# Four of a convolution's 31 taps as products with diagonal matrices

## The chip, the cores and the metric

The kernel runs on one core of a Trainium2 chip. The metric is the device time of one execution in microseconds, median of three runs.

## The reference

Two layers of a transformer for 512 latent and 256 context tokens of 1024 features, in float32. Each layer has a mixer, an output projection with a norm, and a mixture of 32 experts. The first layer's mixer is an attention beside a convolution module, and it is in that module that the change lies:

```python
def _conv_module(u, conv_w, conv_b, ln_g, ln_b):
    a, gate = jnp.split(u, 2, axis=-1)
    glu = a * jax.nn.sigmoid(gate)
    y = lax.conv_general_dilated(glu, conv_w[:, None, :], window_strides=(1,),
                                 padding=[(CONV_WIDTH // 2, CONV_WIDTH // 2)],
                                 dimension_numbers=('NWC', 'WIO', 'NWC'),
                                 feature_group_count=B_WIDTH) + conv_b
    ...
    return jax.nn.silu(yn)
```

Each of the 512 channels is convolved with 31 taps of its own (CONV_WIDTH is 31, B_WIDTH 512), for the latent tokens and the context's; a layer norm over the channels follows.

## The kernel before

Channels lie on the partitions, 128 to a channel tile, four tiles. The tokens of a tile are 784 columns: 512 latent, a gap of 16 zeros, 256 context. A tap is one instruction over 784 columns. Of the 31 taps of a tile, VectorE takes 20 (L746, the first, which also writes the bias, and 19 times L749, which multiplies and adds onto `acc`). The last 11 are products on ScalarE (L756, L759) that GpSimd adds up in `part` (L760); VectorE adds `part` onto `acc` at the end (L768).

The taps are work that fills gaps. `Conv` keeps two lists, `v` for VectorE's taps and `p` for the others, in the order of the channel tiles. `fill(nv, np)` takes so many from the front of each. It is called at fixed points of the program, whatever stands at the front of the lists.

The order of each engine's instructions is the program's own in the stages around the change; a planner orders three engines only in the first layer's output projection and in the second layer's attention (`FREE`). The stages are these.

- `mixer_ab_in`, the loop over the channel tiles (`for ct in range(1, 4)`): TensorE computes the gate of a tile (`ug`, 48 products), ScalarE its sigmoid, TensorE the input (`uu`, 48 products), and VectorE multiplies the two (`glu_of`, L919 and L920), which also puts the tile's taps into the lists (`conv.add`). Four calls `conv.fill(3, 1)` stand in each turn. The same loop splits the pages of weights for the next products: ScalarE writes a rounded high part (L290), VectorE the rest (L295). Channel tile 0 is done before the loop.
- The projection of queries, keys and values, token tile by token tile (`proj`, L695): a tile's products go to PSUM, then a chain on three engines norms, rotates and splits them (`qk_norm`, `qk_rotate`: L347 to L383) and TensorE transposes them a tile later (`qk_trans`). Calls of `fill` stand before the first tile (4), in each `qk_norm` (2) and after each `qk_rotate` (1).
- The first layer's attention (`Attention`): 24 units of two heads by one tile of 128 queries, units 0 to 7 of context tiles, 8 to 23 of latent ones. In each of the first 18 units VectorE takes 1 or 2 taps in turn, between the maxima of the scores (L493) and the scaling of the probabilities (L512). Each second unit also has the products of a chunk of the modulation (`gemv`, L189, L198).

PSUM holds two buffers of 1024 columns (`big`), which `ug`, `uu`, the projections (`qps`) and the attention's scores (`S`) take in turn, and four of 512 (`sm`). The tiles of split keys have the tag `ks` and two buffers, which in the stage before hold two tables (`iota`, `tri`).

Of the kernel before, what the change touches and what calls it, by code (L numbers as in the profile page):

```python
# [7 lines left out]
F32 = mybir.dt.float32  # L8
# [21 lines left out]
PTAPS = 11  # L30
GAP = TAPS // 2
# [8 lines left out]
# engines that do not keep the program's order, by region: 3 is the first layer's output projection, 6 the second's attention  # L40
FREE = {3: [PE, mybir.EngineType.DVE, POOL], 6: [PE, mybir.EngineType.DVE, POOL]}
# pages of the experts' first weights that a layer loads ahead: before the gate, and then at three points of its start
G1 = 3
FIRST = ((11, 0, 2), (7, 3, 2))
# pages beside the lasting ones that a layer's experts have: from the output projection on, and from the experts on
NT = (9, 11)
NS = (9, 3)
# chunks of the second layer's modulation: the tiles at which two are loaded, and how many the attention begins with
M1 = (4, 5)
M2 = 2  # L50
# the row block of the output projection after which the pages that were free before it are taken
# [17 lines left out]
def hybrid_dit_kernel(ctx: ExitStack, tc: tile.TileContext, a, out):  # L69
# [7 lines left out]
    def by_hand(r):  # L77
        """All engines but those given keep the program's order; those take what is ready first."""
        engines = set(ENGINES) - set(FREE.get(r, ()))
        if engines != held[-1]:  # L80
            held.append(engines)
            sched.close()
            sched.enter_context(tc.manual_schedule(engines=engines))
# [13 lines left out]
    class Pages:  # L97
        """Places of 4 KB a partition for weights and other data, each held by one tile after another: what is rounded
        for TensorE's one-pass products and what is not are tiles of their own."""
# [26 lines left out]
    def load(src, n=4, pools=None, queue=nc.sync):  # L126
        """The first n pages of a chunk of weights"""
        w = [pages.new("w", pools=pools) for _ in range(n)]
        for i in range(n):
            queue.dma_start(w[i], src[i])  # L130
        return w

# [31 lines left out]
    def warm(func):  # L164
        """Has ScalarE load the function's table ahead of its use"""
        nc.scalar.activation(keep.tile([128, 1], F32, tag="warm", name="warm", bufs=1), zeros, func)
# [14 lines left out]
    roomy = []  # L181

    def gemv(l, ch, w):
        """Products of a chunk of 512 columns; four column groups of the array take a row block each."""
# [18 lines left out]
    def gemv_first(n, w):  # L203
        """The shift and the scale of a pair of row blocks in layer 0's first norm"""
# [19 lines left out]
    def scale_cols(l, which):  # L224
        """ln gain * (1 + scale), one column a block of 128"""
# [8 lines left out]
    def mod_rows(l, name, src):  # L234
        """A vector of columns as rows in DRAM, to be read into all partitions."""
# [9 lines left out]
    def router_bias(l):  # L245
        """The router's logits of the second norm's shift, and its bias"""
# [12 lines left out]
    def rpow(work, ss, n, scale):  # L259
        """1/sqrt(ss * scale + eps)"""  # L260
# [14 lines left out]
    # A float32 is the sum of two parts of 12 bits each, which TensorE multiplies exactly in one pass each;  # L275
    # a product of two float32 takes three passes then: high * high, high * low and low * high.
    class Split:
        """A chunk of weights in its two parts, made page by page by the steps"""
# [20 lines left out]
        def __call__(self, p, k, o, n):  # L299
            """Columns o to o + n of row block k, part p"""  # L300
            per = PAGE // self.width
            o += k % per * self.width
            return self.parts[p][k // per][:, o:o + n]
# [6 lines left out]
    rope = {}  # L310

    def rope_tables(l, pool, t0=0, n=XT):
        """Of tiles t0 to t0 + n"""
# [17 lines left out]
    # Queries and keys are kept split: a query's two parts below one another on 128 partitions, a key's high part  # L331
    # twice and its low part twice, so that two passes over 128 rows give all four products.
    def qk_norm(l, t, ps, withq, v, work, room=None, fill=lambda n: None):
        """The values of a tile, from the projection in PSUM, and its queries and keys, normed."""
# [21 lines left out]
    def qk_rotate(l, t, n0, qn, W, mid):  # L356
        """Rotation and split of the normed queries and keys"""
# [28 lines left out]
    def keys_of(KS, n):  # L386
        """The tiles that hold the keys of token n, its place there, and how many of the four kinds each holds"""
# [4 lines left out]
    def qk_trans(t, parts, QS, KS):  # L392
        """[token, head dims] -> [head dims, token]"""
# [15 lines left out]
    class Attention:  # L409
        """Units (pair of heads j and j + 4, tile of queries t), three of them in flight: the scores of one,  # L410
        the transposition of the previous one's probabilities, the values of the one before."""
# [47 lines left out]
        def out(self, j, t):  # L459
            """A page holds two tiles of tokens."""  # L460
# [84 lines left out]
    class OutProj:  # L545
        """X += g1 * (feat^T @ w_out), the rms norm of that and the router's logits, tile by tile: a tile's norm
        and logits, and the next tile's features, run beside the products of the tile between them."""
# [89 lines left out]
        def chain_b(self, t, s):  # L637
            """The tile's new rows, transposed, with the second norm's gain"""
# [16 lines left out]
        def chain_c(self, t, s):  # L655
            """The logits: the norm's factor comes after the products, and its shift is in the bias."""
# [6 lines left out]
        def rows_a(self, t, s, eng):  # L663
            """The rows that the experts gather: in layer 0 with the gain and shift, in layer 1 without"""
# [15 lines left out]
    def modulate_T(l, r, h, ps, dst):  # L680
        """Half h of the transposed rows: the second norm's gain and shift, a column of them a block."""
# [9 lines left out]
    def proj(ps, h, tk, w, o, n, ks=range(KT)):  # L691
        """ps[:, o:o+n] = h^T @ w for a tile of tokens"""
# [36 lines left out]
    def col0(t):  # L729
        """A token tile's place among the convolution's columns"""  # L730
        return t * 128 if t < XT else NX + SEP + (t - XT) * 128

    class Conv:
        """The depthwise convolution as work that fills the gaps of VectorE and, for the last PTAPS taps,
        of ScalarE (products) and GpSimd (sums)."""

        def __init__(self, work, glu, acc):
            self.work, self.glu, self.acc = work, glu, acc
            self.v, self.p, self.part, self.started = [], [], {}, set()

        def add(self, ct):
            acc, glu, w = self.acc[:, ct, :], self.glu, lambda i: convp[:, ct, i:i + 1]

            def first():
                self.started.add(ct)
                nc.vector.tensor_scalar(acc, glu[:, ct, 0:CW], w(0), w(TAPS), op0=OP.mult, op1=OP.add)  # L746
# [4 lines left out]
            def ptap(i):  # L751
                if i == TAPS - PTAPS:
# [3 lines left out]
                    nc.scalar.activation(self.part[ct], glu[:, ct, i:i + CW], AF.Copy, scale=w(i))  # L756
# [4 lines left out]

            self.v += [first] + [lambda i=i: tap(i) for i in range(1, TAPS - PTAPS)]
            self.p += [lambda i=i: ptap(i) for i in range(TAPS - PTAPS, TAPS)]

# [86 lines left out]
    def mixer_ab_in(work, mr, xn, hi, v, glu, conv):  # L851
# [33 lines left out]

        tps = {}
# [40 lines left out]
        # channel tile 0, as the blocks of h come  # L927
# [51 lines left out]
        for ct in range(1, 4):  # L979
            w = w0 if ct < 2 else w1  # L980
            ps = big("ug")
            mm_u(ct, 1, ps, w, range(KT))
            conv.fill(3, 1)
# [16 lines left out]
            if ct == 3:  # L1000
                for f in wq.steps:
                    f()
            conv.fill(3, 1)
            glu_of(ct, ps, sig)
# [129 lines left out]
    class Router:  # L1134
        """Each tile's two experts a token and their places among the experts' tokens, tile by tile"""
# [70 lines left out]
        def finish(self):  # L1206
            """The rows that the experts' places take, and where their results go; out of bounds for an empty place,
            as a tile's number is less 64"""
# [16 lines left out]
        def weights(self, work):  # L1225
            """Each assignment's weight: the softmax of the group's logits at their maximum, times that of the two
            experts' logits"""
# [13 lines left out]
        def slots(self, pool, work, room):  # L1241
            """The token and the weight of each place: the tokens of pairs of experts one below the other, those of single
            experts in both halves; out of range and zero for an empty place"""
# [11 lines left out]
            # a weight in three parts of 8 bits, for products in bfloat16 with the places' rows of zeros and a one  # L1255
# [25 lines left out]
        def split(self, pool, w, tok, name):  # L1281
            """Leaves in w the weights of tokens and takes out those of the context's"""
# [6 lines left out]
    # An expert's tokens are taken in blocks of 64: block 0 always, block 1 where the expert has more than 64  # L1289
    # tokens, and the rest, if any expert has more than 128, in a loop of as many steps as that takes.  # L1290
# [22 lines left out]
    class Experts:  # L1313
# [13 lines left out]
        def ahead(self, most=None, spare=0, queue=nc.sync):  # L1327
            """Loads the weights in the order of their use, as far as there are places, but for the spare ones."""
# [27 lines left out]
        def scatter(self, n, b):  # L1356
            """The rows of a block's results, times weight and gate, added to the rows of their tokens. A token's two
            experts are of one group, and order goes round the groups: only every fourth expert can meet a row again."""
# [24 lines left out]
        def scaled(self, dst, yy, w, c):  # L1383
            """Column half c of a block's results, times weight and gate"""
# [7 lines left out]
        def result(self, n, yy):  # L1392
            """The results of an expert's first block, the pair's experts one below the other"""
# [775 lines left out]
```

## Time and profile before

| | |
|---|---|
| median of three runs | 1769.0 us (1768.14 to 1769.58) |
| the profiled execution's span | 1769.0 us |
| TensorE busy | 1567.2 us |
| VectorE busy | 913.2 us |
| ScalarE busy | 528.4 us |
| GpSimd busy | 427.4 us |
| mean granted TensorE clock | 0.966 of full speed |

The profile is of one execution. Engines are PE (TensorE, with PEld its weight loads), DVE (VectorE), ACT (ScalarE), POOL (GpSimd) and SP (the queue that issues most loads). A busy time counts an instruction from its start to its end; matmuls overlap, so a busy TensorE is not one at its peak. In rows of instructions a time in square brackets is the engine's idle time before the instruction, with what ended it. A product of two float32 operands that are not rounded stands as two matmul records.

### The profile page before, as it was taken

Reading aid. Unit: us, or ns where it says so; the run is one execution under the profiler, and the core shown is the slowest. Engines: PE = TensorE matmul, PEld = TensorE weight load, DVE = VectorE, ACT = ScalarE, POOL = GpSimd, SP = SyncE. Lnnn points to the kernel's source line nnn. Section 1 sums busy time; section 2 is a strip of 40 time slices with the busy share of each in tenths; the row PEclk is TensorE's granted clock in tenths of the full one; section 3 lists DMA queues with packets and bytes.
Section 4 is the critical chain, followed back from the end, with each engine's and each line's share of the span. In section 5 each row is a group of like instructions: output and inputs, shape, how many; then the busy total and the mean of one; then the engine's idle time right before and its main releaser. Section 6 shows DMA issues by size and latency. Waiting matters only on the chain. (4 is left out here: it accounts for less than half of the span.)

```text
span 1769.0 us, 24713 instructions
## 1 busy us (share of the span) xinstructions
PE 1567.2 (89%) x8732; PEld 866.9 (49%) x8732; DVE 913.2 (52%) x1747; ACT 528.4 (30%) x1036; POOL 427.4 (24%) x347
## 2 busy tenths in 40 slices
PE   5979689997899999998986789989799999989997
PEld 4867457885333333332321676677334344343442
DVE  3897889788333232322333656656534445344454
ACT  3422468733111111111112434663312122121221
POOL 1535556132112112211111223201121121111110
PEclk9999799999999999999999899999799999999999
DMA  9121743447999999999998338145699999999992
GB/s 368 58 83 66 292 155 122 164 148 278 354 396 397 388 390 386 391 394 389 392 400 332 123 108 319 58 180 188 257 408 408 408 408 406 408 406 406 405 407 91
DMA packets 151597, 519.03 MB, mean 293 GB/s; under 512 B 22445, under 2 KB 23181, under 8 KB 151437
## 3 DMA queue, kind: packets, MB, share of 16 engines
q1 hardware_dynamic: 134300, 479.67, 69.2%
q0 software_dynamic: 11520, 16.81, 3.7%
q10 hardware_dynamic: 5616, 20.45, 3.0%
q8 instruction: 97, 1.59, 0.4%
q14 instruction: 64, 0.52, 0.1%
HBM read 510.49 MB, written 21.02 MB: 300 GB/s over the span
## 5 line engine op out<-in xcount | busy, mean ns | idle before, releaser
L1476 PE MATMUL gu<-w,xt 128*64 128x512 f32 x2304 | 516.7, 597 | 21.1 <-DMA w<-in_ex_dram 11.9
L1476 PEld LDWEIGHTS gu<-w,xt 128*64 128x64 f32 x2304 | 171.5, 137 | 326.6 <-issue 247.6
L1500 PE MATMUL yy<-w,ht 128*64 128x512 f32 x1152 | 264.8, 601 | 14.2 <-PEq L1296 5.9
L1482 DVE TENSOR_TENSOR hh<-hh,gu 128x512 f32<-128x512 f32 x64 | 44.1, 688 | 451.6 <-ACT hh L1481 451.6
L1481 ACT ACTIVATE hh<-gu 128x512 f32<-128x512 f32 x64 | 38.3, 598 | 566.2 <-PEq L1296 416.2
L1500 PEld LDWEIGHTS yy<-w,ht 128*64 128x64 f32 x1152 | 81.4, 137 | 172.4 <-issue 133.7
L1379 POOL DMA_INDIRECT xD<-ys,sidx x40 | 70.6, 1765 | 317.8 <-DVE ys L1375 315.3
L1409 POOL TENSOR_TENSOR lo<-ys,hi 64x1024 fp32r<-64x1024 f32 x29 | 68.2, 2351 | 325.0 <-ACTq L1296 325.0
L749 DVE SCALAR_TENSOR_TENSOR acc<-glu,convp,acc 128x784 f32<-128x784 f32 x76 | 97.9, 1288 | 1.6
L760 POOL TENSOR_TENSOR part<-part,prod 128x784 f32<-128x784 f32 x40 | 84.7, 2118 | 43.2 <-ACT prod L759 42.2
L1375 DVE TENSOR_TENSOR ys<-yy,ys 128x512 f32<-128x512 f32 x64 | 44.3, 692 | 97.8 <-PEq L1296 53.4
L1408 ACT ACTIVATE hi<-ys 64x1024 fp32r<-64x1024 f32 (+1 forms) x35 | 34.4, 983 | 193.1 <-DVE ys L1386 108.8
L1352 POOL DMA_INDIRECT Xg<-hD,gidx x40 | 42.6, 1066 | 188.9 <-PE xtp L1460 179.7
L264 POOL TENSOR_TENSOR rs<-ms,mhalf 128x1 f32<-128x1 f32 (+2 forms) x40 | 41.5, 1038 | 170.8 <-DVE ms L262 170.3
L1390 DVE TENSOR_TENSOR X<-X,cmb 128x512 f32<-128x512 f32 x126 | 77.0, 683 | 1.6 <-PE cmb L1426 1.1
L1426 PE MATMUL cmb<-hi,oh 128*128 128x512 f32 x128 | 58.0, 453 | 22.2 <-DVE oh L1413 20.5
L1460 PEld LDWEIGHTS xtp<-cst,Xg 128*128 128x128 f32 x512 | 58.0, 146 | 34.6 <-PEq L1296 18.6
L1460 PE MATMUL xtp<-cst,Xg 128*128 128x128 f32 x512 | 64.8, 282 | 9.1 <-PEq L1296 9.1
L522 PE MATMUL ptp<-cst,P 128*128 128x128 f32 x368 | 53.3, 284 | 18.7 <-POOL P L510 10.5
L1494 DVE COPY ht<-htp 128x512 f32<-128x512 f32 x64 | 43.8, 684 | 50.0 <-PE htp L1489 50.0
L695 PE MATMUL qps<-wh,hi 128*128 128x256 f32 (+1 forms) x176 | 61.4, 349 | 8.0 <-DVE hi L1819 2.4
L687 DVE TENSOR_SCALAR xt<-xtp,A,modT 128x128 f32<-128x128 f32 x128 | 49.6, 410 | 35.7 <-ACT xt L689 34.6
(310 smaller groups left out, 2633.9 us busy)
## 6 DMA issues: line engine op xcount, KB each, us to landing
w<-in_ex_dram SPq DMA_DIRECT2D x751, 512.0 KB
w<-in_mod_w_dram SPq DMA_DIRECT2D x96, 512.0 KB
w<-in_ex_dram ACTq DMA_DIRECT2D x17, 512.0 KB
w<-in_w_out_dram SPq DMA_DIRECT2D x16, 512.0 KB
w<-in_w_in_ab_dram SPq DMA_DIRECT2D x14, 512.0 KB
hD<-x ACTq DMA_DIRECT2D x8, 512.0 KB
xD<-X ACTq DMA_DIRECT2D x6, 512.0 KB
w<-in_w_in_cd_dram ACTq DMA_DIRECT2D x6, 512.0 KB
```

Of the source, the lines that this page charges most:

```text
L522: nc.tensor.transpose(ps[:, (c - c0) * 128:(c - c0 + 1) * 128], u["P"][c // nk][:, c % nk * 128:(c % nk + 1) * 128], ident)
L687: nc.vector.tensor_scalar(dst[:, k, :], src, g, b, op0=OP.mult, op1=OP.add)
L695: nc.tensor.matmul(ps[:, o:o + n], h(x, k, tk), w(p, k, 0, n), start=(k == 0 and c == 0), stop=(k == KT - 1 and c == 2))
L749: nc.vector.scalar_tensor_tensor(acc, glu[:, ct, i:i + CW], w(i), acc, OP.mult, OP.add)
L760: nc.gpsimd.tensor_tensor(self.part[ct], self.part[ct], t, OP.add)
L1379: return nc.gpsimd.indirect_dma_start(out=xD[:, :], out_offset=bass.IndirectOffsetOnAxis(ap=idx, axis=0), in_=ys[:, :], in_offset=None, bo ...
L1390: nc.vector.tensor_tensor(x, x, ps, OP.add)
L1409: eng.tensor_tensor(lo[rows, c], ys[rows, c], hi[rows, c].bitcast(F32), OP.subtract)
L1426: nc.tensor.matmul(ps, oh[:, tok(t)], y[:, c * 512:(c + 1) * 512], start=(i == 0), stop=(i == 1))
L1460: nc.tensor.transpose(ps[:, k * 128:(k + 1) * 128], src[:, (h * 4 + k) * 128:(h * 4 + k + 1) * 128], ident)
L1476: nc.tensor.matmul(self.gu[c * 64:(c + 1) * 64, b, :], xt[:, k, q * 64:(q + 1) * 64], w[k][:, c * 512:(c + 1) * 512], start=(k == 0), stop ...
L1500: nc.tensor.matmul(yy[c * 64:(c + 1) * 64], t[:, b, f % 2, f // 2, :], w[f][:, c * 512:(c + 1) * 512], start=(f == 0), stop=(f == 3))
```

## The change

Of VectorE's 20 taps of a channel tile, taps 1 to 4 (`ETAPS`) become products on TensorE. For each tap ScalarE writes a diagonal matrix, the identity scaled by the tap's 128 weights, into a tile of the tag `ks` (`diag`, when the channel tile's taps are put into the lists). TensorE multiplies the four diagonals with the shifted columns and accumulates in a `big` buffer (`cps`), 8 products a channel tile. The first vector instruction, before a scalar form that wrote tap 0 and the bias, now multiplies tap 0 and adds the products' sum from PSUM. The bias goes into the first of the other 11 taps, on ScalarE.

The products are issued by `conv.early()`. In the loop this stands behind the gate products of the next channel tile; and the first vector instruction of a tile calls it for what is still unissued. Further, the last `conv.fill(3, 1)` of each turn of the loop is put behind `glu_of` instead of ahead of it. The other lines of the diff only take out comments.

```diff
+ETAPS = 4
...
-            self.v, self.p, self.part, self.started = [], [], {}, set()
+            self.v, self.p, self.e, self.ps, self.part, self.started = [], [], [], {}, {}, set()
...
+            diag = self.room.tile([128, 128 * ETAPS], F32, tag="ks", name="diag", bufs=2)
+            for i in range(ETAPS):
+                nc.scalar.activation(diag[:, tok(i)], ident, AF.Copy, scale=w(i + 1))
+
+            def products():
+                ps = self.ps[ct] = big("cps")
+                for o, n in ((0, 512), (512, CW - 512)):
+                    for i in range(ETAPS):
+                        nc.tensor.matmul(ps[:, o:o + n], diag[:, tok(i)], glu[:, ct, i + 1 + o:i + 1 + o + n], start=(i == 0), stop=(i == ETAPS - 1))
+
             def first():
                 self.started.add(ct)
-                nc.vector.tensor_scalar(acc, glu[:, ct, 0:CW], w(0), w(TAPS), op0=OP.mult, op1=OP.add)
+                self.early()
+                nc.vector.scalar_tensor_tensor(acc, glu[:, ct, 0:CW], w(0), self.ps.pop(ct)[:, 0:CW], op0=OP.mult, op1=OP.add)
...
-                    nc.scalar.activation(self.part[ct], glu[:, ct, i:i + CW], AF.Copy, scale=w(i))
+                    nc.scalar.activation(self.part[ct], glu[:, ct, i:i + CW], AF.Identity, bias=w(TAPS), scale=w(i))
...
-            self.v += [first] + [lambda i=i: tap(i) for i in range(1, TAPS - PTAPS)]
+            self.e.append(products)
+            self.v += [first] + [lambda i=i: tap(i) for i in range(ETAPS + 1, TAPS - PTAPS)]
             self.p += [lambda i=i: ptap(i) for i in range(TAPS - PTAPS, TAPS)]
+
+        def early(self):
+
+            while self.e:
+                self.e.pop(0)()
...
+        conv.room = work
...
             mm_u(ct, 1, ps, w, range(KT))
+            conv.early()
             conv.fill(3, 1)
...
+            glu_of(ct, ps, sig)
             conv.fill(3, 1)
-            glu_of(ct, ps, sig)
```

## Rows read from the trace of the kernel before

**Rows 1.** The page's first part: busy time, share of the span, instructions of each engine.

```profile
PE 1567.2 (89%) x8732; PEld 866.9 (49%) x8732; DVE 913.2 (52%) x1747; ACT 528.4 (30%) x1036; POOL 427.4 (24%) x347
```

**Rows 2.** Busy us by stretch: PE, PEld, DVE, ACT, POOL; granted clock, DMA share, GB/s.

```profile
94.00:116.00 22.00, 15.94 (x80) 13.62 (x79) 21.57 (x19) 7.31 (x9) 8.05 (x4) 0.84 0.00 0
...
260.00:280.00 20.00, 20.00 (x190) 15.47 (x183) 19.56 (x31) 16.86 (x35) 9.28 (x7) 1.00 0.57 213
460.00:900.00 440.00, 421.39 (x2036) 152.38 (x2032) 129.52 (x192) 67.08 (x110) 82.46 (x55) 1.00 1.03 393
```

**Rows 3.** TensorE's timeline, 67 to 134 us: start, duration, line, tiles, idle before.

```profile
67.54 0.51 PE L910 MATMUL uu<-hi,wh 128*128 128x512 f32 x2
...
85.40 0.61 PE L910 MATMUL uu<-hi,wh 128*128 128x512 f32 x2 [0.87 <-DVE glu L920]
...
108.57 1.01 PE L910 MATMUL uu<-hi,wh 128*128 128x512 f32 x2 [6.06 <-DVE glu L920]
...
120.70 0.49 PE L695 MATMUL qps<-wl,hi 128*128 128x512 f32 x1 [1.32 <-DVE wl L295]
...
128.12 0.50 PE L695 MATMUL qps<-wh,hi 128*128 128x512 f32 x1 [1.85 <-DVE glu L920]
...
133.77 0.28 PE L695 MATMUL qps<-wh,hi 128*128 128x256 f32 x1
```

**Rows 4.** VectorE, 60 to 135 us: its taps as a group, then its timeline.

```profile
L749 DVE SCALAR_TENSOR_TENSOR acc<-glu,convp,acc 128x784 f32<-128x784 f32 x34 | 47.5, 1398 | 1.0
...
60.91 0.69 DVE L746 TENSOR_SCALAR acc<-glu,convp 128x784 f32<-128x784 f32 x1
61.63 2.10 DVE L749 SCALAR_TENSOR_TENSOR acc<-glu,convp,acc 128x784 f32<-128x784 f32 x2
...
81.14 3.27 DVE L749 SCALAR_TENSOR_TENSOR acc<-glu,convp,acc 128x784 f32<-128x784 f32 x3
...
85.26 6.21 DVE L749 SCALAR_TENSOR_TENSOR acc<-glu,convp,acc 128x784 f32<-128x784 f32 x3
...
132.14 2.35 DVE L295 TENSOR_TENSOR wl<-w,wh 128x1024 fp32r<-128x1024 f32 x2
```

**Rows 5.** TensorE's timeline at two plain float32 products.

```profile
259.61 1.92 PE L189 MATMUL mps<-w,silu_c 128*32 128x512 f32 x16
...
1116.87 1.09 PE L1978 MATMUL py<-q,pw 128*128 128x512 f32 x2
```

**Rows 6.** Timeline of TensorE and VectorE in the projection.

```profile
141.91 0.51 PE L695 MATMUL qps<-wh,hi 128*128 128x512 f32 x1 [2.32 <-DVE qn L353]
...
162.09 0.95 PE L198 MATMUL mpt<-cst,mrows 128*128 128x2 f32 x8
...
164.17 0.47 PE L695 MATMUL qps<-wh,hi 128*128 128x512 f32 x1
...
165.90 1.03 DVE L749 SCALAR_TENSOR_TENSOR acc<-glu,convp,acc 128x784 f32<-128x784 f32 x1
...
171.50 0.82 DVE L353 TENSOR_TENSOR qn<-qps,rs 128x640 f32<-128x640 f32 x1 [0.79 <-POOL rs L264]
...
195.54 0.77 PE L482 MATMUL S<-low,hi 128*128 128x256 f32 x2 [8.66 <-DVE room L353]
```

**Rows 7.** Attention: a group of VectorE's (227 to 290 us); timeline at units 5, 10, 15, 18.

```profile
L749 DVE SCALAR_TENSOR_TENSOR acc<-glu,convp,acc 128x784 f32<-128x784 f32 x16 | 22.9, 1430 | 0.2
...
196.24 3.64 PE L189 MATMUL mps<-w,silu_c 128*32 128x512 f32 x16
...
226.38 0.75 DVE L493 TENSOR_REDUCE nm<-S 128x1 f32<-128x256 f32 x2
...
257.86 1.80 DVE L493 TENSOR_REDUCE nm<-S 128x1 f32<-128x768 f32 x2
...
285.91 1.81 DVE L493 TENSOR_REDUCE nm<-S 128x1 f32<-128x768 f32 x2
...
302.44 1.82 DVE L493 TENSOR_REDUCE nm<-S 128x1 f32<-128x768 f32 x2 [0.65 <-PE S L482]
```

## What the change will do to the time: the prediction

> **What bounds the kernel now.** The page first: TensorE is busy for 89% of the span and VectorE for 52% [rows 1]. Averages say little about a change in one stretch, so the windows come next. The experts' stretch, from 460 us on, is bound by its weights: the DMA engines are busy throughout [rows 2]. The convolution lies before it. Three stages hold it: the loop over the four channel tiles of the gated input (59 to 128 us), the projection of queries, keys and values (128 to 195), and the first layer's attention (195 to 337). I see nothing that would absorb a shift of these: what the attention's end loses or wins I pass on whole.
>
> In the loop VectorE is the bound. From 94 to 116 us it is busy for 21.57 of 22 us, and TensorE for 15.94 at a granted clock of 0.84 [rows 2]. TensorE's timeline shows it waiting for VectorE four times, 0.87, 6.06, 1.32 and 1.85 us, three times for the gating product that frees a PSUM buffer and once for a page of split weights [rows 3]. So one expects that taking taps from VectorE pays here. But the change does not take them from this loop.
>
> **Where the taps go.** The vector taps are a list, taken from the front at fixed points: 36 in the loop (three rounds of 12), 21 in the projection (4, 2 and five times 3), the rest in the attention. Before, the list has 4 x 20 = 80 entries, so 23 fall to the attention; afterwards 4 x 16 = 64, so 7. Both earlier stages issue as many vector instructions as before. All 16 that go leave the attention: its units 0 to 4 still take 1, 2, 1, 2, 1, and units 5 to 15 take none.
>
> **Price of the products.** Each channel tile gains four products of 512 columns and four of 272, in plain float32. No such accumulating set is in the trace. The nearest: the pool's product of 128 x 128 by 512 columns, one product in two records, 1.09 us with its tail; and the modulation's 16 records, four abreast, 1.92 us, so 0.48 a record with the tail and some 0.43 without [rows 5]. By 0.43: 4 x 2 x 0.43 x (1 + 272/512) = 5.3 us a tile. Upper bound 6.7 (1.09 for each 512), lower 2.6 (one record each); I take 5.3, the nearest row being the same kind of operand. Building the diagonals is 16 ScalarE copies of 128 x 128; ScalarE is busy for 7.31 of 22 us [rows 2] and stands idle after the gate's sigmoid, so they cost nothing; without that cover they'd be about 1 us a tile.
>
> **The loop.** The first vector instruction of tile 0 began at 60.91 [rows 4], and VectorE then worked without a pause. Now it reads the products. Those stand in TensorE's order behind the whole gate batch of the next channel tile, which ended at 67.54 [rows 3], so they end at 67.5 + 5.3 = 72.8. All engines keep the program's order here, and so VectorE stands still for 11.9 us with two split pages, nine taps and the next gating behind it. That is the main cost of the change. Tiles 1 and 2 don't repeat it: their first instruction is 16 and 32 entries down the list, by which time their products are done.
>
> What it costs is bounded from both sides. If VectorE stays the bound, the queue up to the key/value weights' split (ended at 134.5 [rows 4]) comes 11.9 us later, and about 1 more because three first instructions run where two did, without the scalar form's 0.69 us against a tap's 1.05 [rows 4]: +12.9. From this goes contention: three taps took 3.27 us where GpSimd had only small work and 6.21 beside its long additions, and the loop's 34 taps took 47.5, not 34 x 1.05 = 35.7 [rows 4]. Two or three additions now run while VectorE stands, about 1 us each; so +10. If TensorE is the bound: from 67.54 to the key/value product at 133.77 it spent 66.2 us, of which 10.1 waiting and about 2 lost at half clock (the pair after the long wait took 1.01 us, its like 0.61) [rows 3]; 54.1 of work plus 3 x 5.3 is 70.0, +3.8. But it will also wait about 4 us in the second tile's gate batch, whose last split pages VectorE now delivers late: +7.8. Between 7.8 and 10 I take **+8.5** (bounds +3.8 and +12.9). Issuing three taps behind each gating product removes the 6.06 us wait, and that is in these sums.
>
> [...]
>
> **The projection.** VectorE, ScalarE and GpSimd pass one tile after the other through a serial chain, and TensorE follows it (it waited 2.32 us for the normed queries at 141.9 [rows 6]). The fourth channel tile's products are not issued in the loop; the first instruction of tile 3 issues them, entry 49, taken while the fourth token tile is projected. TensorE reaches them at 162.1 by the clock of before and ends at 167.4; the instruction that needs them stood at 165.90 [rows 6]. The diagonals also hold one of two buffers from which the key tiles are split, so that tile's keys wait for the same 167.4. The chain loses 1.5 to 2.6 us; I take **+2.6**. A product tile also takes one of two PSUM buffers; if the fifth projection gets the one freed at about 169 it waits for nothing, TensorE itself being there 2.1 us behind the products (164.17 against 162.09 before [rows 6]), at 169.5.
>
> **The attention.** The 16 taps took 22.9 us of VectorE [rows 7], but not all was in the way. Units 10 to 15 (257.86 to 285.91) took 5.6 us each with taps, units 15 to 18 5.5 without [rows 7], and TensorE was busy for 20.00 of 20 us [rows 2]: nothing to win. Units 5 to 9 took 31.5 us and held eight of the sixteen taps, 11.4 us at their mean of 1.43 [rows 7]. Without them a unit still waits for ScalarE's exponentials, GpSimd's scaling behind its own additions, and TensorE's modulation product; following the queues I find about 0 in unit 5, 1.2 in 6, 1.4 in 7, 0.8 in 8 and 1.8 in 9, where the row vectors' DMA chain starts earlier: **-5.2** (bounds 0 and -11.4; -22.9 if VectorE bounds it all). TensorE waited 8.66 us before the attention [rows 6], and the first modulation product ran at half clock, 3.64 against 1.92 us [rows 5, 7]; the wait falls to about 4. Whether the clock then falls no row says: 6.06 and 8.66 were followed by it, 2.32 was not [rows 3, 6]. I take half: **-0.9**.
>
> **Sum.** The profiled span is 1769.0, as is the median of the three runs. 1769.0 + 8.5 + 2.6 - 5.2 - 0.9 = **1774.0 us**.
>
> **Rivals.** *VectorE was what bound the whole attention.* For it: its queue shows no gap between units 10 and 15. Against: TensorE's full windows and the equal pace of units 15 to 18. If 20 of the 22.9 us come back: 1769 + 11.1 - 20 - 0.9 = 1759. It decides the sign when the attention gives back over 11; chance 0.13, over 1759 to 1765.
>
> *The loop hides the stall.* VectorE catches up and TensorE's sum alone counts: +3.8, and the chain +1.5, the attention -6: 1768. For it: the 10 us of waits that go. Chance 0.25, 1766 to 1771. The change then does nothing that can be measured.
>
> *The buffers turn strictly.* The fifth projection then waits for the fourth tile's queries (171.50 + 2.6 + 0.8 = 174.9 instead of 169.5 [rows 6]); some 3.2 of these 5.4 reach the chain's end: 1777. If the clock halves in the new waits (the loop's 6.06 us wait cost about 2 that way), 1779 to 1781. [...] Chance 0.17.
>
> **How the numbers follow.** My forecast, 1771 to 1777, has 0.45. A measurement of this kernel tells 0.2%, 3.5 us, from no change. Slower than 1772.5: three quarters of the forecast (0.35) and the buffers' 0.17, 0.52. Within: the rest and most of the hidden stall, 0.34. Faster: 0.14. The range for 8 in 10 leaves out the far part of the attention rival and the worst of the clock: 1764 to 1780.
>
> **What would show it.** Right: VectorE idle for about 12 us from 61 us on until products that start near 67.5; product sets of 5.3 us; no 6 us wait before the third gating; the key/value projection starting near 142; keys of the fourth token tile waiting for products; units 5 to 9 some 5 us shorter and units 10 to 15 as long as before. Wrong: products that begin before the gate batch, units 10 to 15 below 5 us, or split weights that are ready when TensorE comes.

## The result and the profile after

| | before | after |
|---|---|---|
| median of four executions | 1768.77 us (1768.14 to 1769.58) | 1780.42 us (1780.13 to 1780.55) |
| span of the profiled execution | 1769.0 us | 1778.5 us (own time 1780.13) |
| granted TensorE clock | 0.966 | 0.967 |

The ratio is 1.0063, with a 95% interval of 1.0049 to 1.0077. By the medians the changed kernel is 11.65 us slower, by the ratio 11.1 (8.7 to 13.6). In the two traces read below the spans differ by 9.5 us. The forecast was 1774.0 us and "slower" as the likeliest sign; the time lies 0.4 us above the end of the range. In the experiments further down, the medians of the first and the fifth leave out one execution each that took half as long again and more (2706.55 and 3060.94 us), for a reason that nothing here shows. In the changed kernel's rows the line numbers differ from those of before: `cps` L753, first vector instruction L758, taps L761, split weights L296, scores L483, maxima L494, modulation L190, `yy` (the experts' second products) L1520.

The page's first part, and the windows that answer to [rows 1, 2]:

```profile
PE 1589.3 (89%) x8796; PEld 877.7 (49%) x8796; DVE 885.6 (50%) x1731; ACT 533.7 (30%) x1052; POOL 425.8 (24%) x347
```
```profile
94.00:116.00 22.00, 22.00 (x110) 17.62 (x110) 21.61 (x21) 5.57 (x9) 8.64 (x4) 0.98 0.00 1
260.00:280.00 20.00, 18.56 (x173) 13.66 (x172) 12.43 (x23) 13.96 (x28) 8.68 (x8) 0.95 0.53 198
```

In the loop TensorE and VectorE are now both full. In the attention VectorE has become light, 12.43 of 20 us against 19.56.

The loop on TensorE's timeline, which answers to [rows 3], and then on VectorE's (two groups and two rows), which answers to [rows 4]:

```profile
67.11 5.43 PE L753 MATMUL cps<-glu,diag 128*128 128x512 f32 x16
...
88.64 1.01 PE L929 MATMUL ug<-hi,wl 128*128 128x512 f32 x2 [2.79 <-DVE wl L296]
...
95.06 5.43 PE L753 MATMUL cps<-glu,diag 128*128 128x512 f32 x16
...
117.17 5.43 PE L753 MATMUL cps<-glu,diag 128*128 128x512 f32 x16
...
150.42 0.50 PE L696 MATMUL qps<-wh,hi 128*128 128x512 f32 x1 [2.67 <-DVE qn L354]
```
```profile
L761 DVE SCALAR_TENSOR_TENSOR acc<-glu,convp,acc 128x784 f32<-128x784 f32 x33 | 41.3, 1251 | 1.0
...
L758 DVE SCALAR_TENSOR_TENSOR acc<-glu,convp,cps 128x784 f32<-128x784 f32 x3 | 3.1, 1025 | 12.0 <-PE cps L753 12.0
...
72.58 1.03 DVE L758 SCALAR_TENSOR_TENSOR acc<-glu,convp,cps 128x784 f32<-128x784 f32 x1 [12.03 <-PE cps L753]
...
149.54 0.82 DVE L354 TENSOR_TENSOR qn<-qps,rs 128x640 f32<-128x640 f32 x1 [0.81 <-POOL rs L265]
```

VectorE stands for 12.03 us at the first instruction of tile 0, for a product set of 16 records and 5.43 us that begins behind the gate batch, as the forecast had it. TensorE no longer waits 6.06 us in the loop, once for 2.79 us instead. The taps are shorter, 1.25 us in the mean against 1.40. The last row, the normed queries of the first token tile, is the mark by which the loop's end is read from here on. On VectorE's timeline of the kernel before it reads:

```profile
141.03 0.82 DVE L353 TENSOR_TENSOR qn<-qps,rs 128x640 f32<-128x640 f32 x1 [0.81 <-POOL rs L264]
```

The projection and the attention, which answer to [rows 6, 7], on TensorE's and VectorE's timelines:

```profile
170.61 5.43 PE L753 MATMUL cps<-glu,diag 128*128 128x512 f32 x16
...
176.53 0.42 DVE L384 TENSOR_TENSOR ks<-qn,ks 128x256 fp32r<-128x256 f32 x1 [1.86 <-ACT ks L381]
176.87 1.02 DVE L758 SCALAR_TENSOR_TENSOR acc<-glu,convp,cps 128x784 f32<-128x784 f32 x1
...
206.45 0.76 PE L483 MATMUL S<-low,hi 128*128 128x256 f32 x2 [5.72 <-DVE room L354]
207.14 3.64 PE L190 MATMUL mps<-w,silu_c 128*32 128x512 f32 x16
...
236.41 0.75 DVE L494 TENSOR_REDUCE nm<-S 128x1 f32<-128x256 f32 x2
...
264.04 1.80 DVE L494 TENSOR_REDUCE nm<-S 128x1 f32<-128x768 f32 x2
...
291.78 1.82 DVE L494 TENSOR_REDUCE nm<-S 128x1 f32<-128x768 f32 x2 [0.18 <-PE S L483]
...
308.52 1.82 DVE L494 TENSOR_REDUCE nm<-S 128x1 f32<-128x768 f32 x2 [0.64 <-PE S L483]
```

Read against the rows of before: the scores are 10.91 us late where the attention begins, unit 5 is 10.03 late, unit 10 is 6.18 late, unit 15 5.87, unit 18 6.08. Behind the attention the output projection begins 6.10 us late (TensorE's timeline, before and then after):

```profile
338.72 0.73 PE L626 MATMUL ops<-wh,fh 128*128 128x512 f32 x2
```
```profile
344.82 0.73 PE L627 MATMUL ops<-wh,fh 128*128 128x512 f32 x2
```

Some 6 us are left, where the sum had 5.0. So far the forecast follows the trace closely. But 6 is not 11.65.

The rest is at the very end. Here is TensorE's timeline at the last expert, first before, then after:

```profile
1742.10 7.09 PE L1476 MATMUL gu<-w,xt 128*64 128x512 f32 x32
1750.70 0.66 PE L1489 MATMUL htp<-cst,hh 128*128 128x128 f32 x4 [1.51 <-DVE hh L1482]
1752.45 3.65 PE L1500 MATMUL yy<-w,ht 128*64 128x512 f32 x16 [1.10 <-DVEq L1296]
...
1761.96 0.40 PE L1426 MATMUL cmb<-lo,oh 128*128 128x512 f32 x1
```
```profile
1745.51 7.09 PE L1496 MATMUL gu<-w,xt 128*64 128x512 f32 x32
1754.11 0.66 PE L1509 MATMUL htp<-cst,hh 128*128 128x128 f32 x4 [1.51 <-DVE hh L1502]
1758.41 6.40 PE L1520 MATMUL yy<-w,ht 128*64 128x512 f32 x16 [3.65 <-PEq L1316]
...
1772.12 0.40 PE L1446 MATMUL cmb<-lo,oh 128*128 128x512 f32 x1
```

The last expert's first products (`gu`) are 3.41 us late, the last product of the kernel (`cmb`) 10.16: 6.75 us are lost in 27. Between the transposes `htp` and `yy` lies a conditional (`when`, L1296 before, L1316 after), which jumps over the code for experts with many tokens. The release is PEq, TensorE's own sequencer: this compare-and-branch took 0.43 us before and 3.43 after, and no other of the 143 on TensorE is above 1 us in either trace. After that wait `yy` ran at a granted clock of 0.50; the windows of the two kernels at that place, before and after, read:

```profile
1752.00:1756.00 4.00, 3.55 (x16) 1.26 (x16) 0.57 (x2) 0.00 (x0) 0.00 (x0) 1.00 0.02 6
```
```profile
1758.00:1762.00 4.00, 3.59 (x10) 1.26 (x12) 0.49 (x1) 0.00 (x0) 0.00 (x0) 0.50 0.02 4
```

No convolution is near. The first question of the experiments is therefore whether this wait belongs to the change at all.

### The profile page after: what moved, and what is told of

The parts are those of the page before. It is cut to its first block, busy times and chain, and to the rows that moved or that the text cites. A ratio compares the mean times of both kernels' runs of the same rounds, so it can differ in the third digit from the quotient of the medians.

```text
span 1778.5 us, 24844 instructions
## 1 busy us (share of the span) xinstructions
PE 1589.3 (89%) x8796; PEld 877.7 (49%) x8796; DVE 885.6 (50%) x1731; ACT 533.7 (30%) x1052; POOL 425.8 (24%) x347
## 5 line engine op out<-in xcount | busy, mean ns | idle before, releaser
L1520 PE MATMUL yy<-w,ht 128*64 128x512 f32 x1152 | 267.5, 606 | 16.9 <-PEq L1316 10.3
L1520 PEld LDWEIGHTS yy<-w,ht 128*64 128x64 f32 x1152 | 81.9, 138 | 177.3 <-issue 138.7
L772 POOL TENSOR_TENSOR part<-part,prod 128x784 f32<-128x784 f32 x40 | 80.3, 2007 | 65.8 <-ACT prod L771 64.8
L761 DVE SCALAR_TENSOR_TENSOR acc<-glu,convp,acc 128x784 f32<-128x784 f32 x60 | 70.9, 1181 | 1.4
```

The source lines that it names most:

```text
L761: nc.vector.scalar_tensor_tensor(acc, glu[:, ct, i:i + CW], w(i), acc, OP.mult, OP.add)
L772: nc.gpsimd.tensor_tensor(self.part[ct], self.part[ct], t, OP.add)
L1520: nc.tensor.matmul(yy[c * 64:(c + 1) * 64], t[:, b, f % 2, f // 2, :], w[f][:, c * 512:(c + 1) * 512], start=(f == 0), stop=(f == 3))
```

## Experiments

Each kernel ran beside the kernel before on the same chip. Medians of before on the three occasions: 1768.32 us for experiments 1 to 4, 1767.63 for 5 to 8, 1769.09 for 9 to 11. Its executions there spread over some 7 to 10 us, so the ratios with their intervals decide.

**1. Instructions alone (`e1_before_pad`).** The kernel before, with products of zeros at its start.

```diff
+        pad = sm("pad")
+        for i in range(32):
+            nc.tensor.matmul(pad[0:1, 0:1], zeros, zeros, start=True, stop=True)
         fin = gemv_first(0, mod[0])
```

> The kernel before, with 32 float32 products of one row and one column added at the very start, where TensorE waits 14.8 us for its first weights: 128 more instructions in TensorE's stream, as the 32 products of the change bring, and none of the convolution's work. In the changed kernel the last conditional of TensorE's sequencer stood for 3.43 us against 0.43 before, and the last expert's second products then ran at the lower clock, 6.40 us against 3.65. Theory A (that wait depends only on where the instructions lie in TensorE's stream): the last conditional again takes about 3.4 us, the last products about 6.4, and the time is some 6 us above the kernel before, 1774 to 1776. The convolution's own cost would then be about 5.5 of the 11.65 us. Theory B (the tail comes of the shift in time that the convolution causes, or of what VectorE and the transfers do then): conditional 0.4, last products 3.65, time 1768 to 1770.

Measured: 1773.24 us, ratio 1.0027 (1.0016 to 1.0038). The 64 added records end at 2.8 us, and TensorE's shift against the trace of before is -0.1 us from there to 240 us; the convolution is untouched. Yet the tail of the changed kernel is there, on TensorE's timeline:

```profile
1750.51 0.66 PE L1492 MATMUL htp<-cst,hh 128*128 128x128 f32 x4 [1.51 <-DVE hh L1485]
1754.80 5.20 PE L1503 MATMUL yy<-w,ht 128*64 128x512 f32 x16 [3.63 <-PEq L1299]
```

The conditional took 3.41 us and `yy` 5.20. Theory A in the mechanism, with a time 0.8 us below its range: the tail is no work of the convolution. It comes of 128 more instructions in TensorE's stream.

**2. The moved taps alone (`e2_move_only`).**

```diff
-            conv.fill(3, 1)
             glu_of(ct, ps, sig)
+            conv.fill(3, 1)
```

> The kernel before with only the second part of the change: three vector taps are issued behind each gating product instead of ahead of it; no diagonals, no products. Theory A (VectorE bounds the loop, and the same instructions are only put in another order): TensorE's wait of 6.06 us at the third channel tile goes, smaller waits for split weights take its place, the key and value projection starts within 1 us of 133.8, and the time is 1767 to 1769. Theory B (the loop is bound by TensorE's waits): the 6 us come back, the key and value projection starts near 128 and the time is near 1764.

Measured: 1769.62 us, ratio 1.0006 (0.9994 to 1.0019): no difference, theory A. The normed queries of the first token tile come at 141.25 against 141.03. Moving the taps neither wins nor costs anything that the interval shows.

**3. Tile 0 does not wait (`e3_tile0_add`).**

```diff
+                if ct == 0:
+                    nc.vector.tensor_scalar(acc, glu[:, ct, 0:CW], w(0), None, op0=OP.mult)
+                    return
                 self.early()
...
+            if ct == 0:
+                self.v.insert(7, lambda: nc.vector.tensor_tensor(acc, acc, self.ps.pop(0)[:, 0:CW], OP.add))
...
-            conv.fill(3, 1)
+            conv.fill(4 if ct == 1 else 3, 1)
```

> The changed kernel, with channel tile 0 begun by the plain scalar form, and its four products added by an instruction of their own at the eighth place of the list: all products stay, VectorE has one instruction more, and nothing stands at the head of its queue for the products. Theory A (the 11.9 us of standing are the cost of the loop): VectorE works from 61 us on, the normed queries of the first token tile come near 142 to 143 instead of 149.5, the attention ends some 6 to 7 us earlier than in the changed kernel, and the time is 1773 to 1776 if the last conditional still takes 3.4 us, 1767 to 1770 if not. Theory B (TensorE's products are the cost, whoever waits for them): normed queries near 148, time 1779 to 1781.

Measured: 1775.28 us, ratio 1.0040 (1.0025 to 1.0055), with a conditional of 3.79 us. VectorE's timeline shows the products added without a pause:

```profile
59.63 0.62 DVE L758 TENSOR_SCALAR acc<-glu,convp 128x784 f32<-128x784 f32 x1
...
67.36 4.65 DVE L764 SCALAR_TENSOR_TENSOR acc<-glu,convp,acc 128x784 f32<-128x784 f32 x3
72.11 0.97 DVE L780 TENSOR_TENSOR acc<-acc,cps 128x784 f32<-128x784 f32 x1
...
142.84 0.82 DVE L354 TENSOR_TENSOR qn<-qps,rs 128x640 f32<-128x640 f32 x1 [0.81 <-POOL rs L265]
```

The first normed queries come at 142.84 (149.54 in the changed kernel), the output projection begins at 339.25 (344.82). Theory A on both, though the attention's end moved by 5.6 us and not by 6 to 7: the stall was 6.7 us of the loop's 8.5. The other 1.8 are left to the products and the added instruction together.

**4. No products in the projection (`e4_not_tile3`).** Diagonals and products only `if ct in (0, 1, 2)`; tile 3 begins with the plain form and keeps its 20 taps.

> The changed kernel without diagonals and products for channel tile 3, whose four taps stay on VectorE: 12 taps are taken instead of 16. Theory A (the fourth tile's products in the middle of the projection, and the buffer of the split keys that its diagonals hold, cost the chain 2.4 us; the four taps that fall back into the attention cost 1.0): the last normed queries come 2.4 us earlier than in the changed kernel, at 203.1, the attention ends 1.4 us earlier, and the time is 1778.5 to 1780 with the last conditional as it is. Theory B (they are hidden): 1780 to 1782.

Measured: 1780.71 us, ratio 1.0072 (1.0057 to 1.0087), conditional 3.40 us. The first scores of the attention behind its wait, on TensorE's timeline:

```profile
203.64 0.77 PE L484 MATMUL S<-low,hi 128*128 128x256 f32 x2 [8.28 <-DVE room L355]
```

They are 2.81 us earlier than in the changed kernel; the output projection begins at 344.12, only 0.7 earlier, since units 5 to 9 take 30.20 us instead of 27.63. The chain's price is as forecast, and the four taps that come back eat most of it. The time lies in theory B's range, but against the changed kernel's 1780.42 the two theories are too close to be told apart by it.

**5. Tiles 1 and 2 alone (`e5_tiles_1_2`).** As experiment 4 with `(1, 2)`, and 48 products of zeros at the start.

> The changed kernel with diagonals and products for channel tiles 1 and 2 alone: tile 0 has no products that VectorE could stand for, tile 3 none in the projection; 8 taps are taken instead of 16. 48 float32 products of one row and one column at the very start move TensorE's stream on, to some 260 instructions more than before. Theory A (the stall of tile 0 and the chain of tile 3 are the costs, and taking taps is worth a little in the attention): normed queries of the first token tile within 1.5 us of 141.0, the attention ends 0 to 2 us earlier than before, time 1766 to 1769 with a last conditional of 0.4 us. Theory B (two sets of products already cost TensorE 5 us in the loop, more than the attention gives back): normed queries near 145, time 1771 to 1773.

Measured: 1776.3 us, ratio 1.0057 (1.0039 to 1.0076), with a short conditional. My theory A failed, and B fell short as well: the first normed queries are at 147.58, 6.5 us late, with half of the products and nothing waiting at tile 0. TensorE's timeline says why:

```profile
102.88 1.01 PE L936 MATMUL ug<-hi,wh 128*128 128x512 f32 x2 [5.19 <-DVE acc L764]
```

Tile 0 keeps 20 taps, so tile 1's first vector instruction is four places later in the list and reads the products at 101.80 us; until then they hold one of the two `big` buffers, and the gate batch of tile 3 waits for it for 5.19 us. It is the rival of the buffers, in the loop where I had not looked for it.

**6. The taps left out (`e6_drop16`).** The kernel before with `range(5, TAPS - PTAPS)` in place of `range(1, TAPS - PTAPS)`: taps 1 to 4 of each tile are not computed.

> The kernel before with the taps 1 to 4 of every channel tile left out, and nothing in their place: part of the convolution is not computed. It shows what taking 16 instructions from VectorE is worth when nothing is paid for it. TensorE's stream is that of before. Theory A (only the units 5 to 9 of the attention are bound by VectorE): the attention ends 4 to 5 us earlier, the units 10 to 15 are as long as before, and the time is 1763 to 1765. Theory B (VectorE bounds the whole attention): it ends 16 to 20 us earlier, time near 1750. Theory C (what the attention's end gains is given back in the experts, whose weights set the pace): 1767 to 1769.

Measured: 1766.06 us, ratio 0.9989 (0.9977 to 1.0001). The maxima of units 5, 10 and 15 on VectorE's timeline:

```profile
225.78 0.74 DVE L493 TENSOR_REDUCE nm<-S 128x1 f32<-128x256 f32 x2
...
252.37 1.80 DVE L493 TENSOR_REDUCE nm<-S 128x1 f32<-128x768 f32 x2
...
280.12 1.82 DVE L493 TENSOR_REDUCE nm<-S 128x1 f32<-128x768 f32 x2 [0.18 <-PE S L482]
```

Units 5 to 9 take 26.59 us against 31.48, units 10 to 14 27.75 against 28.05; the output projection begins 5.6 us earlier, at 333.11. In the attention that is theory A, 0.6 us more at its end than forecast. In the time only some 1.6 us are seen, between A and C, and the interval still holds 0. So a free removal of all 16 instructions is worth at most 0.23%, 4.1 us, and the 5.6 us of the attention's end are not passed on whole.

**7. The changed kernel, moved on in the stream (`e7_after_pad`).** 32 products of zeros at its start.

> The changed kernel with 32 float32 products of one row and one column at the very start, 128 more instructions in TensorE's stream, about 260 more than before. Theory A (the last conditional's 3.4 us depend on where it lies in the stream, and come and go with it): 0.4 us, the last expert's second products 3.65 us, time 1774 to 1776. Theory B (any stream longer than that of before has it): 3.4 us again, time 1780 to 1782.

Measured: 1773.13 us, ratio 1.0038 (1.0024 to 1.0053). TensorE's timeline at the last expert:

```profile
1755.03 0.65 PE L1512 MATMUL htp<-cst,hh 128*128 128x128 f32 x4 [1.51 <-DVE hh L1505]
1756.79 3.65 PE L1523 MATMUL yy<-w,ht 128*64 128x512 f32 x16 [1.10 <-DVEq L1319]
```

With still more instructions the long conditional is gone (0.42 us), and with it the low clock: from 1754 to 1766 us it is 1.00, where the changed kernel has 0.72. What the convolution's change costs is left: 5.5 us by the medians, 6.7 (4.2 to 9.4) by the ratio; the forecast had 5.0.

**8. Products where TensorE is idle (`e8_late_3`).** Only tile 3 has products; they and its first vector instruction stand in the last token tile's `qk_norm`, in the shadow of the wait ahead of the attention.

```diff
+            def taps(n):
+                if i < 5:
+                    return conv.fill(n)
+                conv.fill(n - 1)
+                conv.late()
+
-            Q[i] = qk_norm(0, seq[i], P[i], True, v, work, room, lambda n: conv.fill(n))
+            Q[i] = qk_norm(0, seq[i], P[i], True, v, work, room, taps)
...
+            if i == 4:
+                conv.diagonals()
```

> The changed kernel with diagonals and products for channel tile 3 alone, issued where TensorE waits 8.66 us ahead of the attention, and read by that tile's first vector instruction in the shadow of the same wait; no products in the loop and none in the middle of the projection. Theory A (an idle stretch takes the products for nothing, and TensorE then comes to the attention at the higher clock): no stall in the loop, last normed queries at 194 to 195, the first modulation product 1.9 us instead of 3.64, the attention ends 2 to 4 us earlier than before, time 1764 to 1767 (1769 to 1772 if the last conditional takes 3.4 us here). Theory B (the products hold the PSUM buffer that the first scores want, and the chain loses what the clock gives): 1768 to 1770, or 1773 to 1775 with the long conditional.

Measured: 1771.61 us, ratio 1.0020 (1.0008 to 1.0032), conditional 0.44 us. TensorE's timeline:

```profile
186.74 5.52 PE L757 MATMUL cps<-glu,diag 128*128 128x512 f32 x16
...
195.52 0.50 PE L483 MATMUL S<-low,hi 128*128 128x256 f32 x2 [1.23 <-DVE room L354]
195.95 1.92 PE L190 MATMUL mps<-w,silu_c 128*32 128x512 f32 x16
```

The idle stretch took the products for nothing: 1.23 us of wait are left of 8.66, and the modulation product behind it took 1.92 us instead of 3.64. It brought next to nothing: unit 5 begins at 226.19 against 226.38, and four taps fewer left units 5 to 9 at 31.50 us. Theory A's mechanism is there and its gain is not; the time is outside both ranges, nearer to B's. Why it is 0.2% above the kernel before stays open.

**9. A delay of known length (`e9_delay`).** The kernel before, with seven products behind the attention's last unit.

```diff
         Attention(0, work, units, QS, KS, v, oT, extra, between)
+        pad = sm("pad")
+        for i in range(7):
+            nc.tensor.matmul(pad[:, 0:512], ident, conv.glu[:, i % 4, 0:512], start=True, stop=True)
```

> The kernel before with seven plain float32 products of 512 columns put on TensorE behind the last unit of the first layer's attention; nobody reads them. By the 0.43 us of each record they are 6.0 us, about what the changed kernel is late there (6.1). Theory A (my step: what the attention's end loses is passed on whole): the output projection starts 6 us later, and the time is 1773 to 1775. Theory B (the experts, paced by their weights, give part of it back: in the one pair of traces 6.1 fell to 3.4): 1770 to 1772.

Measured: 1773.76 us, ratio 1.0041 (1.0025 to 1.0057), 4.7 us by the medians, for products of 6.28 us and an output projection that begins 5.58 later:

```profile
337.39 6.28 PE L1120 MATMUL pad<-glu,cst 128*128 128x512 f32 x14
...
344.30 0.71 PE L626 MATMUL ops<-wh,fh 128*128 128x512 f32 x2
```

Theory A: it is passed on, as far as the interval can tell. This kernel's trace is also a warning. Its last `gu` begins at 1741.23, 0.87 us earlier than in the trace of before, as if all had been given back; but that execution took 1769.72 us, the shortest of six. The fall from 6.1 to 3.4 in my pair of traces can be of the same kind, a difference of two single executions, and by itself shows nothing that the experts give back.

**10. Three repairs (`e10_both`).** Tile 0 as in experiment 3, tile 3 as in 4, and 40 products of zeros at the start.

> The changed kernel with three repairs: tile 0 is begun without its products, which are added by an instruction of their own at the eighth place; tile 3 keeps its taps on VectorE; 40 products of one row and one column at the very start bring TensorE's stream to some 260 instructions more than before, where the last conditional was short. Theory A (the three costs stand side by side): normed queries of the first token tile near 143, the last about 2 us later than before, the attention 2 to 4 us shorter, the time 1766 to 1769, not slower than before. Theory B (the products themselves cost TensorE what VectorE saves): the attention ends 2 or more later than before, time 1770 to 1772.

Measured: 1770.64 us, ratio 1.0012 (0.9998 to 1.0026). The first normed queries are at 143.80, the output projection begins 2.7 us later than before: theory B.

**11. Two repairs (`e11_tile0_pad`).** Experiment 3 with 32 products of zeros at the start.

> The kernel in which tile 0 is begun without its products (the third experiment), with 32 products of one row and one column at the very start, as in the seventh. Theory A (the stall and the long conditional add up): the conditional takes 0.4 us, the attention ends near 339 to 340, and the time is 1769 to 1771, some 3 us below the changed kernel with the same 32 products. Theory B (once the conditional is short, the stall is absorbed by the experts): 1772.5 to 1774, as that kernel.

Measured: 1768.87 us, ratio 1.0010 (0.9998 to 1.0022), conditional 0.44 us. The output projection begins 2.4 us earlier than before, some 3 us earlier than I had expected:

```profile
336.32 0.73 PE L627 MATMUL ops<-wh,fh 128*128 128x512 f32 x2
```

Theory A: stall and conditional add up. Each against the kernel before beside it, the ratio is 1.0063 with both, 1.0038 without the long conditional (experiment 7), 1.0040 without the stall (3) and 1.0010 without either: each takes off nearly the same, whether the other is there or not. Without both the change is about even with the kernel before. No version was faster clear of its interval.

## Why the prediction was right in sign and short in time

**The loop, +8.5.** Right, with its mechanism. Normed queries +8.51 (141.03 to 149.54), stall 12.03 for 11.9, product set 5.43 for 5.3. Experiment 3 takes the stall away and gets 6.7 back. Of the two bounds TensorE's was the one that held: it has no wait from 88.64 us to 147 us. But the sum for it was partly lucky. It had a wait of about 4 us in the second tile's gate batch and no half clock behind it. The wait was 2.79 us, the granted clock from 88 to 95 us was 0.51, and the ten pairs of products from 88.64 to 95.06 took 6.42 us, where the ten from 77.28 to 80.77 took 3.49 at a clock of 1.00. The 16 diagonal copies took 0.39 us each on ScalarE, 5.1 us together and so 1.3 a tile, for a forecast of about 1.

**The projection, +2.6.** Right: 10.91 - 8.51 = 2.40 us by the scores; the keys of the fourth token tile waited for the products through ScalarE (1.86 us at 176.53), as forecast. Experiment 4 gives 2.81 back.

**The attention, -5.2.** The mechanism is right, units 5 to 9 alone: 27.63 us against 31.48, so -3.85 in the changed kernel's trace, 27.73 in experiment 3, and 26.59 to 26.60 in experiments 6, 7 and 11, so -4.9. The term was 0.3 to 1.4 us too large; why the traces differ by 1.1 stays open. Units 10 to 14 took 27.74 against 28.05.

**The clock, -0.9.** Unit 5 gained 0.88 on the scores, but not by the clock: the modulation product still took 3.64 us after a wait of 5.72, and where it took 1.92 (experiment 8) unit 5 gained 0.2. The number was right by chance; what gave it is open. Behind the wait of 5.72 us the granted clock was 0.59 from 206 to 212 us.

**"I pass on whole".** For a loss experiment 9 bears it out within its interval. For a gain it does not hold: the attention of experiment 6 ended 5.6 us earlier, for 1.6 us of time and 4.1 at most, and that of experiment 11 ended 2.4 earlier, for none that is seen. Where the gains go stays open; in experiment 6's trace `yy` at the very end alone took 6.66 us instead of 3.65.

**What failed is the sum itself**: "1769.0 + 8.5 + 2.6 - 5.2 - 0.9" takes everything behind the attention as before, but for the shift. It has no term for TensorE's instruction stream, which the change made 128 records longer. That term is 4.8 us (2.8 to 6.7, ratio of experiment 1). With the change's own (experiment 7) it comes to 11.5 of 11.1 by the ratios and to 10.4 of 11.65 by the medians, which the intervals allow. The parts in the trace: conditional +3.0, of which 2.55 reach `yy`, `yy` itself +2.75, the products and the copies behind it the rest of 6.75.

How it depends on the stream shows in the eleven kernels and the two of the change. The sums of matmul and weight-load records on TensorE stand against the kernel before, with the last conditional:

| more records than before | kernels | last conditional |
|---|---|---|
| 0 | before, 2, 6 | 0.43 to 0.44 us |
| 28 to 32 | 9, 8 | 0.43 to 0.44 us |
| 96 | 4 | 3.40 us |
| 128 | after, 1, 3 | 3.41 to 3.79 us |
| 256 | 5, 7, 10, 11 | 0.42 to 0.44 us |

Length alone does not decide: with 256 more records the conditional is as short as with none. The traces also show an instruction packet of 16384 bytes that starts 1.0 us into the long conditional of the changed kernel, at 1755.55 us, and takes 1.04; 1.4 us after its end the branch is over. In all four traces with the long conditional the last instruction packet of this size ahead of it starts 10.3 to 10.5 us before its beginning, and the next one 1.0 to 1.5 us after it. In all nine with the short one such a packet starts 4.6 to 8.0 us before it, and the next when the branch is already over. That the long conditional waited for this packet is my inference: it fits all thirteen traces, and none shows it by itself.

The clock behind the conditional is less strict. `yy` took 5.00 to 6.40 us in the four traces with the long one and 3.65 in seven with the short one, but 6.66 and 5.35 in experiments 6 and 10, where the conditional was short.

## What to carry to other kernels

Count instructions as a term of the sum: in this kernel, which ends in conditionals that jump over code, some hundred instructions at the start of TensorE's stream or in its loop lengthened the last jump by 3 us, and `yy` behind it took 5.00 to 6.40 us each time, for 3.65 before. Test for it with instructions that do nothing, placed where the engine idles, before believing any explanation by the work.

An instruction that reads another engine's result should stand in its queue where that result is ready, and no later than its buffer is wanted: tile 0's, at the head of the queue, cost 6.7 us, and tile 1's, four places further down than in the changed kernel (experiment 5), held its buffer so long that TensorE waited 5.19 us. And work taken off an engine is worth only what the stretch it leaves was bound by: here 3.8 to 4.9 of 22.9 us in the attention, and less in the time.

## What the runs showed that I had not expected

**The clock falls in some executions and not in others.** Near 335 and 382 us nothing of the change is left, and in experiment 2 the wait ahead of the first of these places is as long as before, 1.47 us; the windows of before, then of experiment 2:

```profile
330.00:340.00 10.00, 8.32 (x98) 7.04 (x95) 6.58 (x12) 9.25 (x20) 1.47 (x2) 1.00 0.47 164
380.00:385.00 5.00, 5.00 (x27) 4.10 (x26) 4.83 (x12) 1.16 (x2) 1.59 (x3) 1.00 0.41 167
```
```profile
330.00:340.00 10.00, 8.32 (x89) 7.20 (x85) 5.74 (x11) 8.00 (x16) 1.47 (x2) 0.83 0.42 152
380.00:385.00 5.00, 5.00 (x19) 3.97 (x18) 3.11 (x14) 2.17 (x6) 0.57 (x2) 0.79 0.61 210
```

The first fall cost about 1.5 us (the output projection begins at 340.20 us, for 338.72 before), and some others came and went in the same way, as at `yy` in experiments 6 and 10. It may be one reason why 23 executions of the kernel before lay between 1764.5 and 1774.9 us, and why a difference of 2 us between two traces proves nothing here.

**The PSUM operand cost nothing that the trace shows.** The first vector instruction reads PSUM and takes 1.02 to 1.03 us in all four channel tiles; the tap from SBUF took 1.03 [rows 6].
